# Hybrid attention and recurrent block on one core: the filler's first four output chunks by token halves, and v and differences loaded by pairs of units

## The chip, the cores and the metric

The kernel runs on one core of a Trainium2 chip. The metric is the device time of one execution in microseconds (us), given as the median of several runs. The engines are named as in the profile: PE is TensorE's matmuls and PEld its weight loads, DVE is VectorE, ACT is ScalarE, POOL is GpSimd and SP is SyncE, which here only issues DMAs.

## The reference

The block takes 1024 tokens of width 1024. It normalizes them, projects them once to all inputs of two branches, and joins the branches:

```
h = rmsnorm(x, norm_g) * (1 + scale) + shift
q, k, v, g_attn, xr, g_rnn, m_attn, m_rnn = split(h @ w_in)
y_attn = window_attention(rope(q), rope(k), v, sinks) * silu(g_attn)   # 16 heads of 64, 4 kv heads, window 128
y_rnn  = rg_lru(conv(xr)) * silu(g_rnn)
merged = sigmoid(m_attn) * (y_attn @ w_attn_proj) + sigmoid(m_rnn) * (y_rnn @ w_rnn_proj)
out    = rmsnorm(x + gate * (merged @ w_out), final_g)
```

All of it is float32. Each large matmul is made of three products: an operand is split into a high part h and a remainder l, and h·h, l·h and h·l are summed.

## The kernel before, in words

Tokens lie on the free axis, channels on the 128 partitions. After the normalization comes the input projection, in pairs of column groups (L711); its last pair is still open when attention begins. Then the attention loop runs over 35 steps, `for u in range(32 + 3)`. A unit u is one block of 128 queries of one of four head groups; n = u % 8 is its block. The engines' programs are written out by hand: every call appends to its engine's program, and each engine works through its own in that order.

Step u of the loop puts these on the engines:

- PE: the scores of unit u (`scores`, L1338, 8 matmuls), one piece of filler (12 matmuls), the transposes of unit u-2 (`transposed`, L1372, tile pt), the values of unit u-3 (`values`, L1408, tile pv).
- ACT and DVE: maximum, exponential and division (L1345 to L1365, tile p), then the split of the transposed weights into phc (ACT, L1377) and plc (DVE, L1383).
- POOL: the sinks of unit u+1 (COPY, L1326), the masks of unit u-2 (four selects into pm, L1394, none for a unit with u % 8 = 0), the loads of differences `load_d` (vd) and of values `load_v` (vb) for unit u+1, and, last, whatever remainders wl (L112) are due: `later_d` collects them and `do_later` puts them out at the end of the step. `smr_d` are stores that POOL issues.
- SP: the key and query load of a pair of units, `load_kq(m)`, issued at every odd u for units u+3 and u+4 (tiles ks, 384 KB, and qs, 512 KB). kq2, issued at u = 1, serves units 4 and 5; the loads for units 10 and 12 are issued at u = 7 and 9. All DMA calls go through a helper and have its line, L63.

The filler is a generator, `fill`. Its first six pieces (u = 0 to 5) are the last products of the input projection. `at_slot(s_last + 2, ...)` hangs calls on them, one per piece. From u = 6 on the pieces are those of `rp_steps`: y_rnn @ w_rnn_proj, in 8 output chunks c of 128 channels and for all 1024 tokens. A piece of before, `part(c, kc2)`, does two of the eight contraction chunks kc for one output chunk and both halves of the tokens (L175), so an output chunk takes four pieces. y_rnn lies in DRAM as yh and yl, eight chunks of 512 KB each; `load_y(c)` loads both parts of chunk c, the first two chunks in quarters of 256 KB into tiles that the input projection has left (hha, hla). `load_r(e)` loads the weights of output chunk e as two halves of 256 KB (tile r), and `prep_r(e, i)` splits half i: a cast to wh on ACT (L106) and the remainder wl on POOL while the attention loop runs. Half 0 serves kc 0 to 3, half 1 kc 4 to 7. `finish(c)` copies an output chunk out and stores it. After the attention branch's own filler, `load_b` brings the weights of w_out through a buffer pool, hpool, that also holds the split attention output (`a_alloc`).

The list that hangs loads on the first pieces reads, in before:

```
    at_slot(s_last + 2, ("N", 0, 0, lambda: load_r(0)), ("N", 0, 0, lambda: load_y(0)),
            ("N", 0, 0, lambda: load_r(1)), ("N", 0, 0, lambda: load_y(1)),
            ("N", 0, 0, lambda: prep_r(0, 0)), ("N", 0, 0, lambda: prep_r(1, 0)))
```

Of the kernel before, what the change touches and what calls it, by code (L numbers as in the profile page):

```python
# [13 lines left out]
F32R = mybir.dt.float32r  # L14
# [8 lines left out]
P = 128  # L23
S = 1024
# [31 lines left out]
def tile_hybrid_block(ctx, tc, x, pk, rows, posr, posi, c_row, w_ss, w_gate, w_main, w_v,  # L56
# [14 lines left out]
    def pool(st, name, bufs=1, **kw):  # L71
        return st.enter_context(tc.tile_pool(name=name, bufs=bufs, reuse_waits="tile", **kw))
# [1209 lines left out]
    at_ctx, psx_ctx = ExitStack(), ExitStack()  # L1282
    at = psx = None
    U = {}

    def open_attn():
        nonlocal at, psx
        psm_ctx.close()
        psx = pool(psx_ctx, "psx", space=PSUM)
        W["kq", 1] = pool(at_ctx, "kq1", side="right")  # L1290
        W["pp"] = pool(at_ctx, "pp", bufs=3, side="right")
        W["pp"].tile([P, 64], F32, name="pad", bufs=1)
        W["neg"] = W["pp"].tile([P, 8], F32, name="neg", bufs=1)
        G.memset(W["neg"][:], -1e30)
        for nm in ("vb", "hl", "yo"):
            W[nm] = pool(at_ctx, nm, side="right")
        at = pool(at_ctx, "at", side="right")
        load_kq(1)
        for u in range(4):
            load_v(u)  # L1300
            load_d(u)

# [9 lines left out]
        U["kq", m] = ks, qs  # L1312

    def load_v(u):
        vb = U["v", u] = W["vb"].tile([P, P], F32R, tag="vb", name="vb", bufs=5)
        dma(vb[:], vs_d[u // 8][:, u % 8, :], G)

    def load_d(u):
        if u % 8:
            vd = U["d", u] = at.tile([P, 2, P], F32R, tag="vd", name="vd", bufs=4)  # L1320
            dma(vd[:], dv_d[u // 8][:, u % 8, :, :].unsqueeze(0).to_broadcast([2, 64, 2, P]), G)

    def sink(u):
        px = U["p", u] = W["pp"].tile([P, 4, P + 1], F32, tag="p", name="p")
# [129 lines left out]
    def load_y(c):
        if c < 2:
            hs, ls = [[t[2 * c + i][0] for i in range(2)] for t in (hh, hl)]
            for i in range(2):
                dma(hs[i], yh_d[c][:, SL[i]])
                dma(ls[i], yl_d[c][:, SL[i]])
            yh[c], yl[c] = hs, ls  # L1460
            return
        h_ = W["yp"].tile([P, S], F32R, tag="Y", name="yh")
        l_ = W["yp"].tile([P, S], F32R, tag="Y", name="yl")
        dma(h_[:], yh_d[c])
        dma(l_[:], yl_d[c])
        yh[c] = [h_[:, SL[0]], h_[:, SL[1]]]
        yl[c] = [l_[:, SL[0]], l_[:, SL[1]]]

    def rp_steps():
        h_ctx.close()  # L1470
        pb_ctx.close()
        psr = pool(ps_ctx, "psr", space=PSUM, side="right")
        rp_acc.extend(psr.tile([P, S], F32, name=f"rp{i}") for i in range(2))
        W["yp"] = pool(ctx, "ypool", bufs=12)
        W["tout"] = pool(ctx, "tout", bufs=1)
        W["hpool"] = pool(ctx, "hpool", bufs=6)
# [18 lines left out]
        load_y(2)  # L1495
        load_y(3)
        for i, (c, k) in enumerate(seq):
            part(c, k)
            if i in (1, 2, 3, 4):
                load_y(i + 3)  # L1500
            if i in (1, 2):
                prep_r(i - 1, 1)
            if i in (6, 10):
                finish(0 if i == 6 else 1)
            if i >= 8 and k == 1 and c > 2:
# [10 lines left out]
    def a_alloc():
        U["al", 0] = W["hpool"].tile([P, 2, S], F32R, tag="L", name="al", bufs=1)
        for nm, g in (("ah", 0), ("ah", 1), ("al", 1), ("ah", 2), ("al", 2), ("ah", 3)):
            U[nm, g] = W["hpool"].tile([P, 2, S], F32R, tag="H", name=nm)
        for lst, nm in ((AH, "ah"), (AL, "al")):  # L1520
            lst.extend([[U[nm, g][:, a, t_] for t_ in SL] for a in range(2)]
                       for g in range(NG) if (nm, g) in U)
        t = [W["hpool"].tile([P, HALF], F32R, name="al6", bufs=1)]
        t += [wp.tile([P, HALF], F32R, tag="ws", name="al7", bufs=3) for i in range(3)]
        AL.append([[t[2 * a + i][:] for i in range(2)] for a in range(2)])
# [6 lines left out]
    def a_prep(m):  # L1532

        g, t0 = m // 4, (m % 4) * 256
        y = U.pop(("yq", m))

        def f1():
            gq = U.pop(("gq", m))
            V.tensor_tensor(out=y[:], in0=y[:], in1=gq, op=ALU.mult)

        def f2():
            if not AH:
                a_alloc()
# [12 lines left out]
        return f1, f2, f3  # L1556
# [138 lines left out]
    for u in range(32 + 3):  # L1695
# [233 lines left out]
    wt3 = load_b(4, hpool, "H")  # L1929
# [6 lines left out]
    w22 = load_b(5, hpool, "H")  # L1936
# [134 lines left out]
```

## Time and profile before

| | |
|---|---|
| median of 3 runs | 910.31 us (909.93 to 912.0) |
| the profiled execution's own time | 907.51 us |
| its span, first to last instruction | 905.8 us |
| mean granted TensorE clock | 0.997 |
| PE busy | 891.5 us (98%) |
| DVE, ACT, POOL busy | 718.2, 568.1, 185.1 us |
| DMA | 182.94 MB, mean 202 GB/s |

The page and the views come from one profiled execution. A row of a timeline has its start and length in us, the engine, the line, the operation, the tiles written and read, their shapes, a count, and in square brackets the idle time of the engine just before it with what ended it. The granted clock is a share of full speed. The DMA share is the busy share of the core's 16 DMA engines.

### The profile page before, as it was taken

How to read it: one execution, taken by the hardware profiler on the slowest of the kernel's cores; microseconds unless marked ns; L12 is line 12 of the kernel's file. 1: busy time of each engine (PE TensorE's matmuls, PEld its weight loads, DVE VectorE, ACT ScalarE, POOL GpSimd, SP SyncE). 2: the span in 40 equal slices, each digit the busy share in tenths (PEclk: the TensorE clock that was granted, in tenths of full speed). 3: DMA queues.
4: the chain of work that ended last, by engine and by line, in shares of the span. 5: the costliest groups of instructions: out<-in, count | busy, mean ns of one | idle time of the engine just before them, and what ended most of it. 6: DMA issues, size and time to landing. Idle time of an engine off the chain costs nothing.

```text
span 905.8 us, 12857 instructions
## 1 busy us (share of the span) xinstructions
PE 891.5 (98%) x4314; PEld 746.1 (82%) x4315; DVE 718.2 (79%) x1063; ACT 568.1 (63%) x1098; POOL 185.1 (20%) x331
## 2 busy tenths in 40 slices
PE   9999999999999999999999999998999999999997
PEld 6789888888888888888888888887888888888886
DVE  6988597989859875987789598898999836678855
ACT  7965564655557855786485884887888733115535
POOL 6420241200000000000000002596887720000000
PEclk9999999999999999999999999999999999999999
DMA  9829479873533353354446358999777389416504
GB/s 356 337 69 286 163 257 292 278 218 128 179 134 141 126 208 132 126 181 163 160 143 214 105 198 248 352 340 285 204 226 220 119 302 349 148 61 232 209 1 185
DMA packets 94837, 182.94 MB, mean 202 GB/s; under 512 B 15618, under 2 KB 36114, under 8 KB 94772
## 3 DMA queue, kind: packets, MB, share of 16 engines
q1 hardware_dynamic: 83200, 167.07, 53.4%
q0 software_dynamic: 11424, 14.80, 6.0%
q8 instruction: 34, 0.56, 0.3%
q14 instruction: 31, 0.25, 0.1%
q10 hardware_dynamic: 148, 0.27, 0.1%
HBM read 123.17 MB, written 59.21 MB: 201 GB/s over the span
## 4 chain that ended last, share of the span: by engine, by line
PE 91%; DVE 3%; DMA 3%; ACT 1%; POOL 1%; issue 1%; DVEq 0%; ACTq 0%; SPq 0%
PE bk L711 48%; PE rp L175 13%; PE out L1874 6%; PE pmain L175 5%; PE pgate L1027 5%; PE s_ps L1338 3%; PE bk L487 3%; PE pmain L487 2%; PE pv L1408 2%; DMA r<-w_rp 1%; DMA yl<-yl_d 1%; PE pt L1372 1%; PE pmain L1581 1%; PE pmain L1580 1%; PE pmain L1579 1%; PE bk L258 1%
## 5 line engine op out<-in xcount | busy, mean ns | idle before, releaser
L711 PE MATMUL bk<-nh,wh 128*128 128x512 f32 x368 | 143.3, 389 | 0.0
L711 PE MATMUL bk<-nl,wh 128*128 128x512 f32 x368 | 143.2, 389 | 0.0
L711 PE MATMUL bk<-nh,wl 128*128 128x512 f32 x368 | 98.4, 389 | 0.0
L106 ACT CAST wh<-r 128x512 fp32r<-128x512 f32 x107 | 65.5, 618 | 27.2 <-PE rp L175 12.8
L711 PEld LDWEIGHTS bk<-nh,wl 128*128 128x128 f32 x368 | 69.1, 188 | 14.4
L711 PEld LDWEIGHTS bk<-nh,wh 128*128 128x128 f32 x368 | 69.1, 188 | 14.2
L711 PEld LDWEIGHTS bk<-nl,wh 128*128 128x128 f32 x368 | 69.1, 188 | 14.2
L112 DVE TENSOR_TENSOR wl<-r,wh 128x512 fp32r<-128x512 f32 x91 | 62.0, 689 | 23.3 <-ACT wh L106 23.2
L63 POOL DMA_DIRECT2D yh_d<-av x1 | 0.6, 568 | 357.0 <-ACT av L1094 357.0
L711 PE MATMUL bk<-hl,wh 128*128 128x512 f32 x184 | 71.6, 389 | 0.0
L711 PE MATMUL bk<-hh,wh 128*128 128x512 f32 x184 | 71.6, 389 | 0.0
L112 DVE TENSOR_TENSOR wl<-ws,wh 128x512 fp32r<-128x512 f32 x76 | 52.0, 684 | 11.3 <-ACT wh L106 11.2
L106 ACT CAST wh<-ws 128x512 fp32r<-128x512 f32 x76 | 45.9, 614 | 7.2 <-PE bk L711 3.5
L1358 ACT ACTIVATE p<-p,small 128x129 f32<-128x129 f32 x128 | 50.0, 396 | 0.0
L711 PE MATMUL bk<-hh,wl 128*128 128x512 f32 x184 | 49.2, 389 | 0.0
L1338 PE MATMUL s_ps<-ks,qs 128*128 128x256 f32 (+1 forms) x256 | 35.8, 282 | 4.9 <-DVE yq L1427 3.0
L711 PEld LDWEIGHTS bk<-hh,wl 128*128 128x128 f32 x184 | 34.5, 188 | 7.2
L711 PEld LDWEIGHTS bk<-hh,wh 128*128 128x128 f32 x184 | 34.6, 188 | 7.1
L711 PEld LDWEIGHTS bk<-hl,wh 128*128 128x128 f32 x184 | 34.5, 188 | 7.1
L1338 PEld LDWEIGHTS s_ps<-ks,qs 128*128 128x128 f32 x256 | 32.8, 190 | 7.0 <-DVE yq L1427 3.5
L711 PE MATMUL bk<-hha,wh 128*128 128x512 f32 x92 | 35.8, 389 | 0.0
L711 PE MATMUL bk<-hla,wh 128*128 128x512 f32 x92 | 35.8, 389 | 0.0
(379 smaller groups left out, 2382.3 us busy)
## 6 DMA issues: line engine op xcount, KB each, us to landing
r<-w_main SPq DMA_DIRECT2D x100, 256.0 KB, 4.2
wada<-w_ss SPq DMA_DIRECT2D x16, 512.0 KB, 9.0
qs<-q_d SPq DMA_DIRECT2D x16, 512.0 KB, 7.5
wo_d<-wr SPq DMA_DIRECT2D x28, 256.0 KB, 2.5
wo<-wo_d SPq DMA_DIRECT2D x14, 512.0 KB, 6.2
ks<-k_d SPq DMA_DIRECT2D x12, 384.0 KB, 6.9
xt<-x SPq DMA_DIRECT2D x8, 512.0 KB, 6.8
sma_d<-c SPq DMA_DIRECT2D x16, 256.0 KB, 4.6
```

The costliest lines, as they stand in the source:

```text
L106: A.copy(dst[0][:], src)
L112: eng.tensor_tensor(out=dst[1][:], in0=src, in1=f32(dst[0][:]), op=ALU.subtract)
L175: mm = T.matmul(ps[hf], ww, xx[kc][hf], start=(kc == 0 and ww is w_h and xx is xh), stop=(kc == KC - 1 and xx is xl))
L258: T.matmul(bk[i % 2], zero[:, 0:P], zero, start=True, stop=True)
L487: T.matmul(starts[c][hf], ww[:, c0:c0 + P], xh[kc][hf], start=(kc == 0 and t_ == "h"), stop=(kc == KC - 1 and t_ == "l"))
L711: W["pe"] = T.matmul(ps, ww[:, kc * P:(kc + 1) * P], b[kc][i], start=(first and n == 0), stop=(n == 11), skip_group_check=not first)
L1027: W["pe"] = T.matmul(ps[:, SL[hf]], ww[:, c0:c0 + P], xx_[:, SL[hf]], start=(ic == 0 and i == 0), stop=(ic == 1 and i == 2))
L1338: W["pe"] = T.matmul(o, qs[:, j, qc], ks[:, kb:n % 2 + 2, b, :], start=(b == 0), stop=(b == 1))
L1358: A.activation(px[:, j, :], px[:, j, :], AF.Exp, bias=sm[:, 0, j:j + 1], accum_out=sm[:, 1, j:j + 1])
L1372: W["pe"] = T.transpose(pt[:, :, j, :], px[:, j, 0:P], ident[:])
L1408: W["pe"] = T.matmul(pv[:, cols], w, t_[:, cols], start=(i == 0), stop=(i == len(m) - 1))
L1874: T.matmul(o, a[k][x_][:, p * P:(p + 1) * P], b[k][y_][:, cols], start=(first and k == 0 and i == 0), stop=(k == 3 and i == 2), skip_group ...
```

## The change

There are two edits. No matmul is added or taken away.

First, the filler does output chunks 0 to 3 together. A piece of after, `four(th, p, kc2)`, does two contraction chunks for two output chunks (p = 0: chunks 0 and 1, p = 1: chunks 2 and 3) and one token half th: again 12 matmuls (L1503 to L1505). All of token half 0 comes first, so `load_y(c, th)` loads halves of 256 KB; those of chunks 0 to 3 for th = 0 go into hha and hla. The weights of chunks 2 and 3 stay on the chip over both token halves, in a tile o2 that lies where the attention output will lie later (printed below with a number, o_5945). The loads are hung on earlier pieces: `early(e)` loads the weights of chunk e and the first token half of two y chunks, and both calls come at the first two places of the list above, so their preparations move up two places as well. Chunks 4 to 7 go as before.

Second, from unit 8 on `load_v` and `load_d` load two units at once, at odd u, from a pool vq; for the units 8, 16 and 24 differences are now loaded that nobody reads.

Where hpool was one pool of equal buffers, every buffer now has a name, and `load_b` takes them by a list of names; the order is the same.

The core of the diff:

```diff
+    def load_r(e, halves=(0, 1)):
     def load_v(u):
-        vb = U["v", u] = W["vb"].tile([P, P], F32R, tag="vb", name="vb", bufs=5)
-        dma(vb[:], vs_d[u // 8][:, u % 8, :], G)
+        n, vp = (1, W["vb"]) if u < 8 else (2, W["vq"])
+        vb = vp.tile([P, n, P], F32R, tag="vb", name="vb", bufs=5 if u < 8 else 4)
+        dma(vb[:], vs_d[u // 8][:, u % 8:u % 8 + n, :], G)
...
     def prep_r(e, i):
         def f1():
-            O[e, i] = slot()
+            if e in (2, 3):
+                if e == 2:
+                    W["o2"] = W["hpool"].tile([P, 2, 2, HALF], F32R, tag=("al2", "ah3")[i],
+                                              name="o2")
+                O[e, i] = W["o2"][:, e % 2, 0, :], W["o2"][:, e % 2, 1, :]
+            else:
+                O[e, i] = slot()
...
+        def four(th, p, kc2):
+            for c in (2 * p, 2 * p + 1):
+                acc = rp_acc[p][:, SL[c % 2]]
+                for kc in (2 * kc2, 2 * kc2 + 1):
+                    h, l = O[c, kc // 4]
+                    cols = slice(kc % 4 * P, kc % 4 * P + P)
+                    T.matmul(acc, h[:, cols], yh[kc][th], start=(kc == 0), stop=False)
+                    T.matmul(acc, l[:, cols], yh[kc][th], start=False, stop=False)
+                    W["pe"] = T.matmul(acc, h[:, cols], yl[kc][th], start=False,
+                                       stop=(kc == KC - 1))
...
-        seq = [(c, k) for k in range(4) for c in range(2)]
-        seq += [(c, k) for c in range(2, KC) for k in range(4)]
+        seq = [(p, k, th) for th in range(2) for p, k in (
+            (0, 0), (0, 1), (0, 2), (1, 0), (1, 1), (0, 3), (1, 2), (1, 3))]
+        seq += [(c, k, None) for c in range(4, KC) for k in range(4)]
+        o_at = {0: (1, 1), 1: (2, 0), 2: (3, 0), 4: (2, 1), 5: (3, 1)}
...
-    at_slot(s_last + 2, ("N", 0, 0, lambda: load_r(0)), ("N", 0, 0, lambda: load_y(0)),
-            ("N", 0, 0, lambda: load_r(1)), ("N", 0, 0, lambda: load_y(1)),
+    def early(e):
+        load_r(e)
+        load_y(2 * e, 0)
+        load_y(2 * e + 1, 0)
+
+    at_slot(s_last + 2, ("N", 0, 0, lambda: early(0)), ("N", 0, 0, lambda: early(1)),
             ("N", 0, 0, lambda: prep_r(0, 0)), ("N", 0, 0, lambda: prep_r(1, 0)))
...
-        if 3 <= u < 31:
+        if 3 <= u < 7:
+            load_d(u + 1)
+            load_v(u + 1)
+        if 7 <= u < 30 and u % 2:
             load_d(u + 1)
             load_v(u + 1)
```

Three places show what moves. A row has the line, the operation, the tile written and the tile read, and the shape.

The first is SP's program at the units 0 and 1, around the second key and query load (ks and qs). `r<-w_rp` are weight halves of the recurrent projection, hha and hla the y halves, wo_d and ga_d stores. Before:

```order
L63 DMA r<-w_rp 128x512 x2
L63 DMA wo_d_147<-wr 128x512
L63 DMA ga_d_100<-c 128x2x256
L63 DMA hha_165<-yh_d_117 128x512
L63 DMA hla_167<-yl_d_125 128x512
L63 DMA hha_169<-yh_d_117 128x512
L63 DMA hla_171<-yl_d_125 128x512
L63 DMA ks<-k_d 128x768
L63 DMA qs<-q_d_93 128x1024
L63 DMA r<-w_rp 128x512 x2
```

In the changed kernel the same stretch, from the row behind the first `r<-w_rp`, reads:

```order
L63 DMA hha_165<-yh_d_117 128x512
L63 DMA hla_167<-yl_d_125 128x512
L63 DMA hha_169<-yh_d_118 128x512
L63 DMA hla_171<-yl_d_126 128x512
L63 DMA wo_d_147<-wr 128x512
L63 DMA ga_d_100<-c 128x2x256
L63 DMA r<-w_rp 128x512 x2
L63 DMA hha_173<-yh_d_119 128x512
L63 DMA hla_175<-yl_d_127 128x512
L63 DMA hha_177<-yh_d_120 128x512
L63 DMA hla_179<-yl_d_128 128x512
L63 DMA ks<-k_d 128x768
```

The second pair of weight halves and four y halves, six transfers of 256 KB, now stand ahead of the load instead of behind it.

The second place is POOL's program at the units 7 and 8. Before, it does one remainder (wl) at the end of each unit, of output chunks 0 and 1:

```order
L1326 COPY p<-pk_t 128x4
L1394 AFFINE_SELECT pm<-phc 64x256 x2
L1394 AFFINE_SELECT pm<-plc 64x256 x2
L63 DMA vb<-vs_d_86 128x128
L112 TENSOR_TENSOR wl<-r,wh 128x512
L1326 COPY p<-pk_t 128x4
L1394 AFFINE_SELECT pm<-phc 64x256 x2
L1394 AFFINE_SELECT pm<-plc 64x256 x2
L63 DMA vd<-dv_d_90 128x1x256
L63 DMA vb<-vs_d_86 128x128
L112 TENSOR_TENSOR wl<-r,wh 128x512
```

In the changed kernel the stretch begins with the end of unit 6:

```order
L112 TENSOR_TENSOR wl<-r,wh 128x512 x2
L1333 COPY p<-pk_t 128x4
L1401 AFFINE_SELECT pm<-phc 64x256 x2
L1401 AFFINE_SELECT pm<-plc 64x256 x2
L63 DMA vd<-dv_d_90 128x1x512
L63 DMA vb<-vs_d_86 128x256
L112 TENSOR_TENSOR o_5945<-r,o_5945 128x512
L1333 COPY p<-pk_t 128x4
L1401 AFFINE_SELECT pm<-phc 64x256 x2
L1401 AFFINE_SELECT pm<-plc 64x256 x2
L112 TENSOR_TENSOR o_5945<-r,o_5945 128x512
```

The remainders of chunks 0 and 1 have moved to the end of unit 6, both at once; units 7 and 8 make those of chunks 2 and 3, and unit 8 has no loads.

The third place is PE's program in unit 9, the fourth piece of `rp_steps`, behind that unit's scores. Before, the piece goes on with output chunk 1, and its weights are those that were split two units earlier:

```order
L1338 MATMUL s_ps<-ks,qs 128x256 x8
L175 MATMUL rp_5778<-yh,wh 128x512 x2
L175 MATMUL rp_5778<-yh,wl 128x512 x2
L175 MATMUL rp_5778<-yl,wh 128x512 x2
L175 MATMUL rp_5778<-yh,wh 128x512 x2
L175 MATMUL rp_5778<-yh,wl 128x512 x2
L175 MATMUL rp_5778<-yl,wh 128x512 x2
L1372 MATMUL pt<-ident,p 128x2x64 x4
```

In the changed kernel the piece begins chunks 2 and 3. L1504 is the product with the remainder; the first six filler rows are of chunk 2, the next two of chunk 3:

```order
L1345 MATMUL s_ps<-ks,qs 128x256 x8
L1503 MATMUL rp_5778<-hha_165,o_5945 128x512
L1504 MATMUL rp_5778<-hha_165,o_5945 128x512
L1505 MATMUL rp_5778<-hla_167,o_5945 128x512
L1503 MATMUL rp_5778<-hha_169,o_5945 128x512
L1504 MATMUL rp_5778<-hha_169,o_5945 128x512
L1505 MATMUL rp_5778<-hla_171,o_5945 128x512
L1503 MATMUL rp_5778<-hha_165,o_5945 128x512
L1504 MATMUL rp_5778<-hha_165,o_5945 128x512
```

The second and the eighth filler matmul of unit 9 now read the remainders that stand at the ends of units 7 and 8 on POOL.

More of the change, by code (lines that the diff above doesn't have):

```diff
@@ L1296, in open_attn @@
             W[nm] = pool(at_ctx, nm, side="right")
-        at = pool(at_ctx, "at", side="right")
+        at = pool(at_ctx, "at", bufs=2, side="right")
         load_kq(1)
-        for u in range(4):
+        load_v(0)
+        for u in range(1, 4):
             load_v(u)
@@ L1314, in load_v @@
     def load_v(u):
-        vb = U["v", u] = W["vb"].tile([P, P], F32R, tag="vb", name="vb", bufs=5)
-        dma(vb[:], vs_d[u // 8][:, u % 8, :], G)
-    def load_d(u):
-        if u % 8:
-            vd = U["d", u] = at.tile([P, 2, P], F32R, tag="vd", name="vd", bufs=4)
-            dma(vd[:], dv_d[u // 8][:, u % 8, :, :].unsqueeze(0).to_broadcast([2, 64, 2, P]), G)
+        n, vp = (1, W["vb"]) if u < 8 else (2, W["vq"])
+        vb = vp.tile([P, n, P], F32R, tag="vb", name="vb", bufs=5 if u < 8 else 4)
+        dma(vb[:], vs_d[u // 8][:, u % 8:u % 8 + n, :], G)
+        for i in range(n):
+            U["v", u + i] = vb[:, i, :]
+    def load_d(u):
+        n, dp = (1, at) if u < 8 else (2, W["vq"])
+        vd = dp.tile([P, n, 2, P], F32R, tag="vd", name="vd", bufs=4)
+        dma(vd[:], dv_d[u // 8][:, u % 8:u % 8 + n, :, :].unsqueeze(0).to_broadcast(
+            [2, 64, n, 2, P]), G)
+        for i in range(n):
+            U["d", u + i] = vd[:, i, :, :]
     def sink(u):
@@ L1432, in tile_hybrid_block @@
     rp_acc, R, O = [], {}, {}
-    def load_r(e):
+    def load_r(e, halves=(0, 1)):
         src = w_rp[e] if e < KC else w_ap[e - KC]
-        R[e] = [load_half(src[:, SL[i]]) for i in range(2)]
+        for i in halves:
+            R[e, i] = load_half(src[:, SL[i]])
     later_a, later_d = [], []
@@ L1441, in f1 @@
         def f1():
-            O[e, i] = slot()
-            cast(O[e, i], R[e][i])
+            if e in (2, 3):
[5 more added lines that the diff above has]
+                O[e, i] = slot()
+            cast(O[e, i], R[e, i])
         later_a.append(f1)
-        later_d.append(lambda: rest(O[e, i], R[e][i], eng=G if "att" in W else V))
+        later_d.append(lambda: rest(O[e, i], R[e, i], eng=G if "att" in W else V))
         if "att" not in W:
@@ L1452, in do_later, with load_y @@
                 todo.pop(0)()
[L1454 to L1467, printed above, removed]
+    def load_y(c, th):
+        if c < 4 and not th:
+            h_, l_ = hh[c][0], hl[c][0]
+            yh[c], yl[c] = [h_], [l_]
+        elif c < 4:
+            if c % 2 == 0:
+                W["y1"] = [W["yp"].tile([P, S], F32R, tag="Y", name=n_) for n_ in ("yh", "yl")]
+            h_, l_ = [t[:, SL[c % 2]] for t in W["y1"]]
+            yh[c].append(h_)
+            yl[c].append(l_)
+        else:
+            if not th:
+                for y_, n_ in ((yh, "yh"), (yl, "yl")):
+                    t = W["yp"].tile([P, S], F32R, tag="Y", name=n_)
+                    y_[c] = [t[:, t_] for t_ in SL]
+            h_, l_ = yh[c][th], yl[c][th]
+        dma(h_, yh_d[c][:, SL[th]])
+        dma(l_, yl_d[c][:, SL[th]])
     def rp_steps():
@@ L1487, in f @@
                 A.copy(t[:], rp_acc[c % 2][:])
-                store(tr_d[c], t[:])
+                if th is None:
+                    store(tr_d[c], t[:])
+                else:
+                    for a in range(2):
+                        store(tr_d[2 * c + a][:, SL[th]], t[:, SL[a]])
             later_a.append(f)
@@ L1491, in finish @@
                 do_later()
-        seq = [(c, k) for k in range(4) for c in range(2)]
-        seq += [(c, k) for c in range(2, KC) for k in range(4)]
[L1495 to L1505, printed above, removed]
+        seq = [(p, k, th) for th in range(2) for p, k in (
+            (0, 0), (0, 1), (0, 2), (1, 0), (1, 1), (0, 3), (1, 2), (1, 3))]
+        seq += [(c, k, None) for c in range(4, KC) for k in range(4)]
+        y_at = {0: (6, 0), 1: (7, 0), 2: (0, 1), 3: (1, 1), 4: (2, 1), 5: (3, 1),
+                6: (4, 1), 7: (5, 1), 9: (6, 1), 10: (7, 1)}
+        r_at = {0: (3, 0), 1: (2, 1), 2: (3, 1)}
+        o_at = {0: (1, 1), 1: (2, 0), 2: (3, 0), 4: (2, 1), 5: (3, 1)}
+        out_at = {5: (0, 0), 8: (1, 0), 13: (0, 1), 17: (1, 1)}
+        prep_r(0, 1)
+        load_r(2, (0,))
+        load_y(4, 0)
+        load_y(5, 0)
+        for i, (c, k, th) in enumerate(seq):
+            if th is None:
+                part(c, k)
+            else:
+                four(th, c, k)
+            if i in y_at:
+                load_y(*y_at[i])
+            if i in r_at:
+                load_r(r_at[i][0], r_at[i][1:])
+            if i in o_at:
+                prep_r(*o_at[i])
+            if i in out_at:
+                finish(*out_at[i])
+            if i >= 20 and k == 1:
                 finish(c - 1)
-            if i % 4 == 2:
+            if i % 4 == 2 and i >= 10:
                 load_r((i + 2) // 4 + 1)
-            if i >= 4 and i % 4 < 2:
+            if i >= 12 and i % 4 < 2:
                 prep_r((i + 4) // 4, i % 4)
@@ L1514, in tile_hybrid_block, with a_alloc @@
     AH, AL = [], []
[L1516 to L1525, printed above, removed]
+    def a_alloc(g):
+        for nm in ("ah", "al"):
+            if nm == "al" and g == 3:
+                t = [W["hpool"].tile([P, HALF], F32R, name="al6")]
+                t += [wp.tile([P, HALF], F32R, tag="ws", name="al7", bufs=3) for i in range(3)]
+                AL.append([[t[2 * a + i][:] for i in range(2)] for a in range(2)])
+                continue
+            t = U[nm, g] = W["hpool"].tile([P, 2, S], F32R, tag=f"{nm}{g}", name=nm)
+            (AH if nm == "ah" else AL).append([[t[:, a, t_] for t_ in SL] for a in range(2)])
     def load_gq(m):
@@ L1541, in f2 @@
         def f2():
-            if not AH:
-                a_alloc()
+            if len(AH) == g:
+                a_alloc(g)
             A.copy(U["ah", g][:, :, t0:t0 + 256], y[:])
@@ L1755, in tile_hybrid_block @@
     at_ctx.close()
+    vq_ctx.close()
     psx_ctx.close()
@@ L1775, in tile_hybrid_block, with load_b @@
     ahh, alh = [[lst[c // 2][c % 2] for c in range(KC)] for lst in (AH, AL)]
-    in_l = []
-    def load_b(j, pool, tag):
+    places = [nm + str(g) for g in range(NG) for nm in ("ah", "al")][:7] * 2
+    def load_b(j, pool, tag=None):
         res = []
         for i in range(2):
-            if pool is hpool:
-                in_l.append(len(in_l) in (1, 8))
-                tag = "L" if in_l[-1] else "H"
             r = tpool.tile([P, 2, HALF], F32, tag="wr", name="wo32", bufs=2)
             dma(r[:], wo_d[j][2 * i:2 * i + 2].rearrange("k p n -> p k n"))
-            t = pool.tile([P, 2, 2, HALF], F32R, tag=tag, name="wo",
-                          bufs=1 if tag == "L" else None)
+            t = pool.tile([P, 2, 2, HALF], F32R, tag=tag or places.pop(0), name="wo")
             A.copy(t[:, 0], r[:])
@@ L1911, in result @@
         dma(out[t * P:(t + 1) * P, :], xo[t][:])
-    w21 = load_b(1, hpool, "H")
+    w21 = load_b(1, hpool)
     for t in range(4):
         load_x(t)
-    wt2 = load_b(2, hpool, "H")
+    wt2 = load_b(2, hpool)
     for p in range(4):
```

15 lines of the change are left out of this document (8 added, 7 removed).

## The prediction

> **What bounds the kernel now.** The busy line of the page comes first.
>
> ```profile
> span 905.8 us, 12857 instructions
> PE 891.5 (98%) x4314; PEld 746.1 (82%) x4315; DVE 718.2 (79%) x1063; ACT 568.1 (63%) x1098; POOL 185.1 (20%) x331
> ```
>
> TensorE works 891.5 of 905.8 us, so a change that keeps the matmuls, as this one does, can only move its 14.3 us of idle time. The windows of the attention loop tell where some of that lies (columns: window, its length, busy us of PE, PEld, DVE, ACT, POOL, granted clock, DMA share, GB/s).
>
> ```profile
> 557.00:590.00 33.00, 32.55 (x190) 28.20 (x190) 26.44 (x48) 24.82 (x79) 15.86 (x32) 1.00 1.04 337
> 590.00:625.00 35.00, 30.33 (x181) 25.86 (x180) 29.69 (x51) 26.08 (x83) 27.07 (x46) 1.00 1.06 329
> 625.00:700.00 75.00, 74.95 (x455) 65.60 (x454) 70.74 (x124) 65.10 (x204) 58.48 (x107) 1.00 0.75 219
> ```
>
> The clock is full. From 557 to 625 the DMA engines are busy throughout (share 1.04 and 1.06) and PE loses 0.45 and 4.67 us; from 625 on it loses nothing. The waits of PE in 557 to 625 give the releasers, and its timeline the places: the scores of units 4, 10 and 12.
>
> ```profile
> PE s_ps L1338 <- DVE yq L1427: 3.0, 1, 3.0
> PE s_ps L1338 <- DMA qs<-q_d: 1.4, 1, 1.4
> PE s_ps L1338 <- DVE p L1365: 0.5, 1, 0.5
> PE rp L175 <- DMA yl<-yl_d: 0.2, 1, 0.2
> ```
>
> ```profile
> 574.91 1.19 PE L1338 MATMUL s_ps<-ks,qs 128*128 128x256 f32 x8 [0.45 <-DVE p L1365]
> ...
> 606.02 1.19 PE L1338 MATMUL s_ps<-ks,qs 128*128 128x256 f32 x8 [1.37 <-DMA qs<-q_d]
> ...
> 618.76 1.19 PE L1338 MATMUL s_ps<-ks,qs 128*128 128x256 f32 x8 [3.04 <-DVE yq L1427]
> ```
>
> The wait of 3.04 is put down to VectorE, but the query transfers decide it. The two that units 10 and 12 read were issued, and landed, thus:
>
> ```profile
> 591.64 0.32 SPq L63 DMA_DIRECT2D qs<-q_d  x1
> DMA to landing us min/median/max: 14.2/14.2/14.2
> ```
>
> ```profile
> 607.18 0.32 SPq L63 DMA_DIRECT2D qs<-q_d  x1
> DMA to landing us min/median/max: 11.4/11.4/11.4
> ```
>
> 591.64 + 14.2 = 605.8, and unit 10 starts at 606.02; 607.18 + 11.4 = 618.6, and unit 12 starts at 618.76. Both queries came late through a full DMA, and the 0.22 us for yl is of the same kind.
>
> **Part 1: the second query and key load (kq2) goes behind six more transfers.** Unit 4 reads kq2. The change puts both weight halves of chunk 1 and the four y halves of chunks 2 and 3 ahead of it on SP, 6 x 256 KB = 1.573 MB, which stood behind it. SP's timeline, the landings, and the DMA rate:
>
> ```profile
> 566.67 0.32 SPq L63 DMA_DIRECT2D ks<-k_d  x1
> 568.48 0.32 SPq L63 DMA_DIRECT2D qs<-q_d  x1
> 569.29 1.40 SPq L63 DMA_DIRECT2D r<-w_rp  x2
> ```
>
> ```profile
> ks<-k_d SPq DMA_DIRECT2D x1, 384.0 KB, 6.9
> r<-w_rp SPq DMA_DIRECT2D x1, 256.0 KB, 6.2
> ```
>
> ```profile
> 568.00:570.00 2.00, 2.00 (x14) 1.72 (x13) 1.90 (x5) 1.94 (x8) 0.01 (x1) 1.00 1.07 384
> 570.00:572.00 2.00, 2.00 (x13) 1.78 (x13) 1.93 (x5) 1.60 (x5) 0.18 (x1) 1.00 1.03 396
> 572.00:574.00 2.00, 2.00 (x12) 1.68 (x12) 1.86 (x5) 2.00 (x8) 0.00 (x0) 1.00 1.00 366
> ```
>
> ks landed at 573.6, and the r behind qs at 569.29 + 6.2 = 575.5; its 256 KB take 0.7 us at the mean of 382 GB/s, so qs landed at about 574.8. Unit 4's scores began at 574.91, with PE free since 574.46: no slack at all. With 1.573 MB more ahead, kq2 lands 1.573 / 0.382 = 4.1 us later, and unit 4 waits **+4.1 us**. Nothing covers it: scores lead their unit, and PE runs in program order. Bounds: 4.7 us at the 337 GB/s of 557 to 590; below, 0, if the six do not delay kq2 (a rival below). I take 4.1, the rate of the very stretch.
>
> [...]
>
> **Part 2: two remainders that GpSimd makes too late for unit 9.** In the changed order the fourth filler step (unit 9) is the first on chunks 2 and 3, and its second and eighth matmuls read remainders (L112) that GpSimd makes at the ends of units 7 and 8, behind masks and loads. The rows of GpSimd and their neighbours:
>
> ```profile
> 600.54 0.65 POOL L1326 COPY p<-pk_t 128x4 f32<-128x4 f32 x1
> 601.15 0.89 POOL L1394 TENSOR_SCALAR_AFFINE_SELECT pm<-phc 64x256 fp32r<-64x256 f32 x2
> 602.10 0.89 POOL L1394 TENSOR_SCALAR_AFFINE_SELECT pm<-plc 64x256 fp32r<-64x256 f32 x2
> 602.94 0.83 POOL L63 DMA_DIRECT2D vd<-dv_d  x1
> 603.76 0.56 POOL L63 DMA_DIRECT2D vb<-vs_d  x1
> ```
>
> ```profile
> L112 POOL TENSOR_TENSOR wl<-r,wh x18: 1262/1294/1802, 583.7 to 733.0; 128x512 fp32r<-128x512 f32 x18
> ```
>
> ```profile
> 590.25 0.57 ACT L1377 CAST phc<-pt 128x512 fp32r<-128x512 f32 x1
> ```
>
> ```profile
> 584.85 0.95 PE s_ps L1338 x8
> 585.81 2.75 PE rp L175 x12
> ```
>
> ```profile
> 599.63 0.64 PE L1338 MATMUL s_ps<-ks,qs 128*128 128x256 f32 x4
> ```
>
> Per unit GpSimd needs 0.6 for the copy, 1.8 for four masks, 1.4 for the two loads, and 1.3 per remainder. Count from the start of unit 6 (584.85). The masks can start when the cast phc ends, at 590.82, so at 6.0. Unit 6 now ends with two remainders: 6.0 + 1.8 + 1.4 + 2.6 = 11.8. Unit 7: copy, masks, pair loads, remainder, 5.1, to 16.9. Unit 8, without loads: 0.6 + 1.8 + 1.3 = 3.7, to 20.6. PE reaches unit 9's scores at 599.63, so 14.8, its second filler matmul after 0.95 + 0.23 (2.75 / 12) at 16.0, and the eighth six matmuls (1.37) later at 17.3. GpSimd delivers at 16.9 and 20.6, so PE ends 20.6 - 17.3 = **+3.3 us** late. Below: if unit 8's masks wait for nothing but their own cast, it is 9.9 (unit 8, two thirds of 14.8) + 6.0 + 1.8 + 1.3 = 19.0, so 1.7. Above: all four remainders at the longest, 1.80, add 2.0, so 5.3. I take 3.3, from the median row. A pair load is costed as one issue: the 256 KB stores in the next fence issue in 0.55 each, no more than the smaller vb, so size does not set it.
>
> ```profile
> 591.25 1.10 POOL L63 DMA_DIRECT2D smr_d<-c  x2
> ```
>
> **Part 3: the same at unit 12.** The seventh step (unit 12) reads at its eighth matmul the remainder queued at the end of unit 11, again behind that unit's masks and loads. In before the same chain stands in unit 11:
>
> ```profile
> 614.65 0.60 PE L1372 MATMUL pt<-ident,p 128*128 128x128 f32 x4
> ```
>
> ```profile
> 620.23 1.30 POOL L112 TENSOR_TENSOR wl<-r,wh 128x512 fp32r<-128x512 f32 x1
> ```
>
> It ends at 621.53, 6.9 us after unit 11's transposes. PE, without its wait of 3.04, would be at the scores of unit 12 at 615.72, 1.1 after them, and at the eighth matmul after 1.1 + 0.95 + 0.23 + 1.37 = 3.6. So **+3.3 us**. Below: the bare work of GpSimd, 5.1, gives 1.5; above, a remainder of 1.80 gives 3.8.
>
> **Part 4: what goes.** Ahead of unit 10's query stand 256 KB less (0.7 us), ahead of unit 12's 1.573 MB less (4.1 us), since output chunks 0 to 3 first need only half of each y. PE also comes 4.1 and 7.4 us later than its old pace. So 1.37 + 3.04 + 0.22 go: **-4.6 us**. Late next are the remainders above.
>
> **At nothing.** The filler keeps 16 steps of 12 matmuls for the first four chunks, at the same 0.23 each. Pair loads spare GpSimd 1.4 us in every even unit from 8 on; after 625 it lies beside PE, which is full. If that cover went, nothing would be lost, as GpSimd only does less. The unused differences of units 8, 16 and 24 are 0.39 MB, 1.0 us of DMA where its share is 0.75; uncovered, at most that. The y halves are more issues at 0.32 on SP, less than the 0.7 that 256 KB take to move.
>
> **Sum.** 4.1 + 3.3 + 3.3 - 4.6 = +6.1. The profiled execution took 907.51 (span 905.8): 913.6. The median of the runs, 910.31, lies 2.8 above it: **916.4**.
>
> **Rivals.**
> - *Everything hidden, so faster.* The six transfers do not hold up kq2, and GpSimd delivers by 16.0 and 17.3. Of the waits only 1.37 - 0.7 = 0.7 at unit 10 stays, as PE comes on time: -3.9, 906.4. It decides wherever the new waits together stay below 2 us. For it: the wait at unit 4 before is booked on p, not on a transfer. Against it: a DMA share of 1.0 ahead of unit 4, and a GpSimd with 11.8 us of work by the end of unit 6. Chance 0.14.
> - *kq2 in time, GpSimd late.* The transfers in flight are not served in turn, so the six do not cost kq2 their whole length: 3.3 + 3.3 - 4.6 = +2.0, 912.3. Against it: ks, issued at 566.67, landed at 573.6 and r, issued 2.6 later, at 575.5, in turn. Chance 0.15. [...]
> - *kq2 late, GpSimd in time.* The 4.1 us at unit 4 let GpSimd get ahead, or the masks run earlier than in the rows: 4.1 - 4.6 = -0.5, 909.8. Against it: the remainders of unit 8 wait for a cast made in unit 8. Chance 0.16.
> - *As forecast*: 0.55.
>
> **How the numbers follow.** A measurement of this kernel can tell 0.2%, 1.8 us, from no change. The low ends, with kq2 in time, are 0 + 1.7 + 1.5 - 4.6 = -1.4, 908.9; the high ends 4.7 + 5.3 + 3.8 - 4.6 = +9.2, 919.5. The range 908.9 to 919.5 leaves out the first rival, 0.14, and little else. Faster than 908.5: the first rival and a fifth of the third, 0.17. Within 908.5 to 912.1: the rest of the third and a third of the second, 0.18. Slower: the rest, 0.65.
>
> **What would show it.** Right: unit 4's scores wait 4 us for qs; SP's kq2 has the six transfers ahead of it; in unit 9 the lines that replace L175 wait about 1 us and then 2 us for GpSimd's remainder, in unit 12 about 3 us; no wait for qs at units 10 and 12. Wrong: unit 4 starts at 575, so part 1 falls; no wait of PE for GpSimd, so parts 2 and 3 fall; or units 10 and 12 still wait for queries, so part 4 does. The whole is wrong if the idle of PE in 557 to 640 is below the 5.1 us of before.

## The result and the profile after

| | before | after |
|---|---|---|
| median | 910.31 us | 920.17 us (918.47 to 920.3) |
| the profiled execution's own time | 907.51 us | 920.09 us |
| its span | 905.8 us | 918.0 us |
| mean granted clock | 0.997 | 0.994 |

The ratio is 1.0114, interval 1.01 to 1.0128: the change is slower by 10.4 us by the ratio, by 9.9 us between the two medians. The forecast was slower by 6.1, with 919.5 as the upper end. A fourth run of the kernel before, 991.15 us, lies 80.8 us above the median of the other three and is left out.

The busy line of the page shows the first surprise. PE has the same 4314 matmuls as before, but is busy for 895.9 us, where it was 891.5. Of the 12.2 us by which the span grew, 7.8 are idle time of PE and 4.4 are matmuls that took longer.

```profile
PE 895.9 (98%) x4314; PEld 748.3 (82%) x4315; DVE 721.1 (79%) x1063; ACT 567.4 (62%) x1098; POOL 170.2 (19%) x310
```

The list of waits of TensorE (PE) in 557 to 640 us of the changed kernel has those that were forecast, and no others but 0.2 us. The queries of units 10 and 12 are gone from it.

```profile
PE rp L1504 <- POOL o L112: 6.0, 3, 3.0
PE s_ps L1345 <- DMA qs<-q_d: 5.5, 1, 5.5
PE pv L1415 <- POOL pm L1401: 0.2, 1, 0.2
```

PE's timeline has them at unit 4's scores, at the second and the eighth filler matmul of unit 9, and at the eighth of unit 12:

```profile
579.40 2.05 PE L1345 MATMUL s_ps<-ks,qs 128*128 128x256 f32 x8 [5.54 <-DMA qs<-q_d]
...
610.34 0.50 PE L1504 MATMUL rp<-hha,o 128*128 128x512 f32 x1 [1.13 <-POOL o L112]
...
613.94 0.51 PE L1504 MATMUL rp<-hha,o 128*128 128x512 f32 x1 [1.94 <-POOL o L112]
...
631.79 0.50 PE L1504 MATMUL rp<-yh,o 128*128 128x512 f32 x1 [2.98 <-POOL o L112]
```

Unit 4's eight score matmuls took 2.05 us, where they took 1.19 before. The windows of the same stretch show that it ran at a lower clock (window, length, busy us of PE, PEld, DVE, ACT, POOL, granted clock, DMA share, GB/s). The clock column is no longer 1.00 throughout.

```profile
557.00:590.00 33.00, 27.45 (x141) 23.47 (x140) 20.05 (x35) 18.95 (x61) 10.81 (x22) 0.90 0.86 268
590.00:625.00 35.00, 31.54 (x185) 26.38 (x185) 30.18 (x50) 27.21 (x87) 25.59 (x44) 1.00 1.00 303
625.00:640.00 15.00, 12.01 (x62) 10.10 (x61) 10.95 (x21) 9.11 (x29) 6.76 (x13) 0.89 0.81 256
```

Cut at the moments at which the clock changes, the two drops look thus:

```profile
575.08:578.50 3.42, 0.00 (x0) 0.00 (x0) 0.81 (x2) 0.58 (x1) 3.16 (x7) 1.00 1.02 340
578.50:581.91 3.41, 2.51 (x10) 2.45 (x11) 0.00 (x0) 0.43 (x1) 0.82 (x1) 0.50 1.08 401
581.91:585.32 3.41, 3.41 (x9) 2.64 (x9) 3.09 (x6) 1.70 (x9) 0.00 (x0) 0.50 0.60 165
585.32:588.74 3.42, 3.42 (x25) 3.12 (x25) 1.32 (x3) 1.64 (x4) 1.09 (x4) 1.00 0.04 14
```

```profile
629.70:633.11 3.41, 1.32 (x6) 1.04 (x7) 2.44 (x4) 1.52 (x7) 1.97 (x3) 1.00 0.92 271
633.11:636.52 3.41, 3.41 (x18) 3.41 (x17) 0.79 (x2) 1.32 (x3) 0.94 (x3) 0.50 0.72 254
636.52:639.93 3.41, 3.41 (x20) 2.87 (x20) 3.20 (x7) 2.14 (x9) 0.89 (x3) 1.00 0.67 228
```

A stretch of 3.41 us in which PE worked 0.00 or 1.32 us is followed by half clock, for two stretches the first time and one the second. In the kernel before, the longest wait, 3.04 us, fell across two such stretches (edges in steps of 3.413 us from a drop of its clock at 23.46 us; another, at 904.10, is 258 such steps behind that), and with 1.75 and 2.04 us of work in them the clock stayed full:

```profile
613.97:617.39 3.42, 1.75 (x10) 1.14 (x8) 3.25 (x6) 2.86 (x10) 1.73 (x4) 1.00 1.05 296
617.39:620.80 3.41, 2.04 (x13) 1.90 (x14) 2.14 (x5) 0.94 (x4) 2.88 (x6) 1.00 1.08 282
```

GpSimd (POOL) in the changed kernel made its remainders late, as was worked out: the two of unit 6 in one go, then those that units 9 and 12 wait for. Masks of unit 7 (pm) stand between them; the second row of them, shown here, took 1.57 us, where the prediction's row has 0.89.

```profile
601.66 2.98 POOL L112 TENSOR_TENSOR wl<-r,wh 128x512 fp32r<-128x512 f32 x2
...
606.03 1.57 POOL L1401 TENSOR_SCALAR_AFFINE_SELECT pm<-plc 64x256 fp32r<-64x256 f32 x2
...
609.02 1.26 POOL L112 TENSOR_TENSOR o<-r,o 128x512 fp32r<-128x512 f32 x1
...
612.62 1.26 POOL L112 TENSOR_TENSOR o<-r,o 128x512 fp32r<-128x512 f32 x1
...
630.47 1.26 POOL L112 TENSOR_TENSOR o<-r,o 128x512 fp32r<-128x512 f32 x1
```

### The profile page after: what moved, and what is told of

The parts are those of the page before. It is cut to its first block, busy times and chain, and to the rows that moved or that the text cites. A ratio compares the mean times of both kernels' runs of the same rounds, so it can differ in the third digit from the quotient of the medians.

```text
span 918.0 us, 12851 instructions
## 1 busy us (share of the span) xinstructions
PE 895.9 (98%) x4314; PEld 748.3 (82%) x4315; DVE 721.1 (79%) x1063; ACT 567.4 (62%) x1098; POOL 170.2 (19%) x310
## 5 line engine op out<-in xcount | busy, mean ns | idle before, releaser
L711 PEld LDWEIGHTS bk<-nl,wh 128*128 128x128 f32 x368 | 69.6, 189 | 14.3
L106 ACT CAST wh<-r 128x512 fp32r<-128x512 f32 x103 | 63.0, 618 | 28.6 <-PE pmain L175 9.6
L711 PE MATMUL bk<-hl,wh 128*128 128x512 f32 x184 | 71.6, 389 | 0.0
L711 PE MATMUL bk<-hh,wh 128*128 128x512 f32 x184 | 71.6, 389 | 0.0
L1384 ACT CAST phc<-pt 128x512 fp32r<-128x512 f32 x32 | 18.7, 586 | 32.5 <-PE pv L1415 16.3
```

The source lines that it names most:

```text
L106: A.copy(dst[0][:], src)
L711: W["pe"] = T.matmul(ps, ww[:, kc * P:(kc + 1) * P], b[kc][i], start=(first and n == 0), stop=(n == 11), skip_group_check=not first)
L1384: A.copy(phc[:], U["t", u][0])
```

## The experiments

Each was timed against runs of the kernel before on the same chip (medians of it 909.06, 909.52, 909.25 and 908.38 in the four sessions). The changed kernel itself was timed only in the first session, with 910.31 for the kernel before, so a gain against its 920.17 is read from two sessions; the ratios to the kernel before are the safer measure. Two theories stood against each other for the size: the waits bring half clock with them, or something else in the change costs the rest.

**1. kq2 first.** The second `early` call and chunk 1's preparation go behind the second query and key load.

```diff
-    at_slot(s_last + 2, ("N", 0, 0, lambda: early(0)), ("N", 0, 0, lambda: early(1)),
-            ("N", 0, 0, lambda: prep_r(0, 0)), ("N", 0, 0, lambda: prep_r(1, 0)))
+    at_slot(s_last + 2, ("N", 0, 0, lambda: early(0)), ("N", 0, 0, lambda: None),
+            [("N", 0, 0, lambda: early(1)), ("N", 0, 0, lambda: prep_r(0, 0))],
+            ("N", 0, 0, lambda: None), ("N", 0, 0, lambda: prep_r(1, 0)))
```

> The changed kernel with the second early call (weights of chunk 1, first token half of y chunks 2 and 3) put behind the second query and key load, and chunk 1's preparation two pieces later. Theory A (kq2 lands late behind six transfers, and the idle time of 5.5 us lets the granted clock fall to half for 6.8 us): the wait for qs at unit 4 (5.54) falls to about 0.45 and the half clock behind it goes, so 5.1 + 2.7 = 7.8 us less than the changed kernel's 920.2: 912.4. Theory B (the half clock has another cause than that wait): 5.1 less, 915.1. Theory C (kq2 is not late because of the six): no change, 920.

Measured 913.01 (912.78 to 913.3), ratio 1.0042 (1.0027 to 1.0058): 7.2 us less than the changed kernel, or 6.5 by the two ratios. The time alone lies between theories A and B; the trace is A's. PE waits 1.1 us for qs instead of 5.5, and the same 6.0 for the remainders, so that part is independent. The drop behind unit 12 is left: half clock from 626.09 to 629.50, behind a stretch with 1.34 us of work. That none is left at units 4 and 5 is an estimate from the mean granted clock of the profiled execution, 0.997 where the changed kernel has 0.994.

```profile
PE rp L1504 <- POOL o L112: 6.0, 3, 2.9
PE s_ps L1345 <- DMA qs<-q_d: 1.1, 1, 1.1
```

**2. The remainders of chunks 2 and 3 on VectorE.**

```diff
-        later_d.append(lambda: rest(O[e, i], R[e, i], eng=G if "att" in W else V))
+        later_d.append(lambda: rest(O[e, i], R[e, i], eng=G if "att" in W and e not in (2, 3) else V))
```

> The changed kernel with the four remainders of output chunks 2 and 3 made by VectorE instead of GpSimd. Theory A (units 8, 9 and 12 wait for a GpSimd that is late): the waits for the remainders (6.0 in all), unit 8's loss of 1.5 and the half clock behind unit 12's wait (1.9) go, 9.5 less; the four subtractions of 0.69 on VectorE cost between 0 and 2.8: 910.7 to 913.5. Theory B (TensorE would be late there anyway, for the casts or for the queries): less than 4 us gained, 916 or more.

Measured 916.88 (913.97 to 918.78), ratio 1.0083 (1.0063 to 1.0102): 3.3 us gained (2.8 by the ratios), where theory A wanted 6.7 to 9.5. The profile is of an execution of 913.97 us, the lowest of six. In it the wait of unit 12 for a remainder is gone, but VectorE is late too for unit 9, and a wait of 1.1 us for the query of unit 12 came back:

```profile
PE s_ps L1345 <- DMA qs<-q_d: 6.0, 2, 4.9
PE rp L1504 <- DVE o L112: 2.1, 1, 2.1
```

So another engine alone does not remove the waits. Unit 8's loss, which I had put down to these four, stayed as well (unit 8 to 9 took 6.26 us, 6.28 in the changed kernel, 4.77 before): the two remainders of unit 6, on which it rests, are of chunks 0 and 1 and were still on GpSimd.

**3. Both.**

> Both edits together. Theory A: 920.2 - 7.8 - 9.5 + (0 to 2.8) = 902.9 to 905.7, faster than the kernel before by 5 to 7 us. Theory B (a faster TensorE runs into the queries of units 10 and 12 again): a wait for qs of 0.7 or more returns there, 906 to 910.

Measured 910.09 (908.11 to 911.07), ratio 1.0006 (0.9996 to 1.0017), 4 us above theory A and level with the kernel before. It lies at the upper end of theory B, but without B's sign, as no wait for qs is left. PE waits 3.5 us for VectorE's remainders, and a stretch with 2.1 us of idle time (1.30 us of work) is again followed by half clock, from 607.3 to 610.8 us.

```profile
PE rp L1504 <- DVE o L112: 3.5, 2, 2.1
PE s_ps L1345 <- DVE plc L1390: 1.2, 1, 1.2
```

**4. Work in the wait.** The changed kernel with idle matmuls ahead of unit 4's scores, on the keys and queries of the pair before; the scores overwrite what they write.

```diff
+        if u == 4:
+            ko, qo = U["kq", 1]
+            for i in range(36):
+                T.matmul(s_ps[:, i % 4, :], qo[:, i % 4, 0:P], ko[:, 0:2, 0, :],
+                         start=True, stop=True)
```

> The changed kernel with 36 more matmuls of the scores' shape ahead of unit 4's scores; they read keys and queries of the pair before and write what the scores overwrite. They fill 36 x 0.12 = 4.3 us of the 5.5 us in which TensorE waits for qs. Theory A (the idle time itself lowers the clock): the granted clock stays at 1.00 through units 4 and 5, and though there is more work, the time falls by 2.7 us, to 917.5. Theory B (something else lowers it): no gain, 920 or more.

Measured 917.96 (915.98 to 922.32), ratio 1.0095 (1.0075 to 1.0115). 2.2 us less, but with a range too wide to tell, and the theory's own sign is missing. The profile, of an execution of 922.32, has the clock falling to half at unit 4 still, behind a stretch with 1.21 us of work, as 2.2 us of wait remained in it:

```profile
577.97:581.38 3.41, 1.21 (x10) 1.03 (x10) 0.00 (x0) 0.00 (x0) 1.66 (x2) 1.00 1.05 346
581.38:584.79 3.41, 3.41 (x12) 2.83 (x11) 1.76 (x3) 2.14 (x9) 0.00 (x0) 0.50 0.88 287
```

So I filled the whole wait, with 52 (`range(52)` in the diff):

> As the fourth experiment, with 52 instead of 36 idle matmuls ahead of unit 4's scores: 52 x 0.12 = 6.2 us, more than the whole wait. Theory A (a stretch of the clock's grid with some 2 us of idle time lowers the clock): no half clock at units 4 and 5, scores 0.9 us later than in the changed kernel, unit 5 at 585.2 instead of 587.0, so 1.8 us less than 920.2: 918.4, with more work. Theory B (the half clock is not the answer to idle time): 0.9 us more, 921.

Measured 919.04 (917.06 to 920.08), ratio 1.0099 (1.0079 to 1.0119). The time alone does not settle it; the windows and the timeline do. From 573 to 587 us PE has no idle time, the clock stays full, and unit 5's scores start at 584.97, where 585.2 was expected and 587.04 is the changed kernel's: 2.1 us earlier with 52 matmuls more. So idle time is what lowers the clock there: with 0.00 us of work in a stretch it was 0.50 in the changed kernel, with work throughout 1.00.

```profile
576.50:580.00 3.50, 3.50 (x31) 3.44 (x29) 0.00 (x0) 0.00 (x0) 2.84 (x4) 1.00 1.02 374
580.00:583.50 3.50, 3.50 (x21) 3.08 (x20) 1.51 (x3) 2.13 (x9) 0.00 (x0) 1.00 0.90 268
```

```profile
584.97 1.12 PE L1350 MATMUL s_ps<-ks,qs 128*128 128x256 f32 x8
```

The same scores in the changed kernel:

```profile
587.04 1.12 PE L1345 MATMUL s_ps<-ks,qs 128*128 128x256 f32 x8
```

The profiled execution, at 920.08, is no faster for it: the clock fell again behind a later wait and was 0.50 from 613.38 to 616.79, behind a stretch with 1.51 us of work, where the changed kernel has 1.00. The waits for remainders are the same 6.0 us, but they fell otherwise on the 3.41 us stretches: in the changed kernel the least work in one at unit 9 was 1.66 us, from 609.22 to 612.63.

**5. Preparation one step earlier.** This is the first experiment, and in addition chunks 0 and 1 get their second halves prepared at units 3 and 5, and chunks 2 and 3 theirs one unit earlier; all remainders stay on GpSimd.

```diff
-        o_at = {0: (1, 1), 1: (2, 0), 2: (3, 0), 4: (2, 1), 5: (3, 1)}
+        o_at = {0: (2, 0), 1: (3, 0), 3: (2, 1), 4: (3, 1)}
-        prep_r(0, 1)
...
+            ("N", 0, 0, lambda: prep_r(0, 1)), ("N", 0, 0, lambda: prep_r(1, 0)),
+            ("N", 0, 0, lambda: prep_r(1, 1)))
```

> The changed kernel with kq2 ahead of the second early call, as in the first experiment, and with the preparation of the second halves of chunks 0 and 1 and of both halves of chunks 2 and 3 one step earlier; the remainders stay on GpSimd, which stood idle for 7.2 us at unit 5. Theory A (the remainders are late only because they are queued late): from the 913.0 of the first experiment go unit 8's loss (1.6), the waits of unit 9 (3.1) and unit 12 (2.9) and the half clock behind it (1.9): 903.5, faster than the kernel before by 5. Theory B (a faster TensorE meets the queries of units 10 and 12 or the casts again): up to 5 of the 9.5 come back, 904 to 909. Theory C (GpSimd is short of time, not late in order): no better than 911.

Measured 909.02 (907.15 to 911.52), ratio 0.9997 (0.9985 to 1.0009): theory B's time, though not by the waits that it named. No wait for a remainder is left, so the order on GpSimd was the point; but a new wait stands there, for the values of a pair load:

```profile
PE pv L1415 <- DMA vb<-vs_d: 3.3, 1, 3.3
PE pv L1415 <- POOL pm L1401: 0.9, 2, 0.7
```

**6. The six transfers alone, in the kernel before.**

```diff
-    at_slot(s_last + 2, ("N", 0, 0, lambda: load_r(0)), ("N", 0, 0, lambda: load_y(0)),
-            ("N", 0, 0, lambda: load_r(1)), ("N", 0, 0, lambda: load_y(1)),
+    at_slot(s_last + 2, [("N", 0, 0, lambda: load_r(0)), ("N", 0, 0, lambda: load_y(0))],
+            [("N", 0, 0, lambda: load_r(1)), ("N", 0, 0, lambda: load_y(1))],
+            ("N", 0, 0, lambda: None), ("N", 0, 0, lambda: None),
```

> The kernel before, with nothing changed but that the loads of chunk 1's weights and of y chunk 1 stand ahead of the second query and key load instead of behind it: the same six transfers. Theory A: unit 4 waits 5 us for qs, the half clock adds 2.7 or 1.3 by where the wait falls in the clock's windows, and the old waits of units 10 and 12 (4.6) are swallowed, as the transfers gain what TensorE loses: +1.8 to +3.2, 911 to 912.3. Theory B (the queries of units 10 and 12 stay late): +6.4 to +7.8, 915.5 to 917. Theory C (the order of the loads does not matter): 909.1.

Measured 915.33 (912.72 to 917.63), ratio 1.0066 (1.0049 to 1.0084), 6.0 us more: between the theories, closer to B. Unit 4 waits 6.2 us, and the clock is half from 577.06 to 587.30, as expected. Of the old waits unit 10's is swallowed, unit 12's is not, so that PE comes later is not enough to remove that one. Nor do fewer bytes ahead of it seem enough: in experiment 2, where the bytes are those of the changed kernel and PE is less late, 1.1 us of it came back.

```profile
PE s_ps L1338 <- DMA qs<-q_d: 6.2, 1, 6.2
PE s_ps L1338 <- DVE yq L1427: 3.1, 1, 3.1
```

**7. The pair loads alone, in the kernel before** (the diff's `load_v`, `load_d` and their calls).

> The kernel before with values and differences loaded by pairs of units from unit 8 on, alone. Theory A: TensorE never waits for GpSimd there, so nothing: 909.1, within 0.2%. [...] Theory C (the unused differences and the larger transfers press on a full DMA, and the queries of units 10 and 12 come later): 0.5 to 1 us slower.

Measured 913.46 (913.2 to 914.48), ratio 1.0046 (1.0033 to 1.0059): 4 us slower, more than any theory had. The second edit is not free. Unit 12's query, issued at 606.7 (607.2 in the kernel before), now lands after 16.1 us instead of 11.4. The mean granted clock of the profiled execution is 0.995, that of the kernel before 0.997, and the wait for the query grows from 3.0 to 6.6:

```profile
PE s_ps L1345 <- DMA qs<-q_d: 6.6, 1, 6.6
```

A pair's difference load, the first, takes 16.9 us from issue to landing:

```profile
vd<-dv_d POOLq DMA_DIRECT2D x1, 256.0 KB, 16.9
```

**8. The same bytes at the same places, as single transfers.** The lines are against experiment 7; tiles and transfers are again of one unit each.

```diff
-            load_d(u + 1)
-            load_v(u + 1)
+            for w in (u + 1, u + 2):
+                load_d(w)
+                load_v(w)
```

> The kernel before with the loads of the pair version at the same places, with the same bytes (unused differences too), but each unit's load as a DMA of its own. Theory A (the form matters: a pair's transfer is slow and holds up the others): like the kernel before, 909.5. Theory B (bytes asked for one unit earlier press on a full DMA ahead of unit 12's query): like the pair version, 913.5.

Measured 910.6 (909.63 to 912.05), ratio 1.0016 (1.0006 to 1.0025): 1.4 us, nearer to A. About a third of the cost of pairs is that bytes are asked for earlier; about two thirds go when each unit's load is a transfer of its own. Unit 12's query lands after 13.2 us here. The two single difference loads land after 12.6 us:

```profile
vd<-dv_d POOLq DMA_DIRECT2D x2, 128.0 KB, 12.6
```

**9. Single loads in the changed kernel.**

> The changed kernel with values and differences loaded singly again, as before. Theory A (a queue on GpSimd sets units 9 and 12): unit 8's end has two more issues of 1.4 us ahead of the remainder that unit 9 waits for, so +1.4; unit 11 has as many as it had: 921.6. Theory B (GpSimd is not what unit 9 waits for, or a pair costs what two singles cost): no change, 920.2.

Measured 921.11 (920.49 to 921.56), ratio 1.0127 (1.0113 to 1.0142). The mechanism is there (the second wait of unit 9 grows from 1.94 to 3.39 us, all three waits for remainders from 6.0 to 6.6), but the intervals of this and of the changed kernel overlap, so the size is not settled. In the changed kernel pair loads are neither clearly better nor clearly worse.

**10. Experiment 5 with single loads.**

> The fifth experiment (kq2 first, preparation one step earlier) with values and differences loaded singly. Theory A (a pair load lands late and is what TensorE waited for there, 3.3 us for vb and 0.9 for masks): 4 us less than its 909.0, 905, faster than the kernel before by about 4.5; the two more issues in even units cost GpSimd 1.4 us, which the earlier preparation leaves room for. Theory B (the wait only moves on, to the queries of units 10 and 12): 908 to 909.5.

Measured 904.58 (904.05 to 906.86), ratio 0.9951 (0.9935 to 0.9966): theory A to half a microsecond. It is the first version faster than the kernel before, by 4.5 us, and it no longer has the second edit. PE loses 1.2 and 1.4 us in the two stretches, and the clock is full in both:

```profile
557.00:590.00 33.00, 31.81 (x185) 27.44 (x184) 27.03 (x46) 25.55 (x80) 18.04 (x34) 1.00 1.04 328
590.00:625.00 35.00, 33.65 (x200) 28.89 (x198) 33.20 (x57) 29.74 (x94) 30.07 (x51) 1.00 1.07 323
```

**11. y chunk 1 behind kq2 too**, to take away the last wait for qs at unit 4 (1.1 us).

> The version with kq2 first, earlier preparation and single loads, with one step more of the same: the two halves of y chunk 1 also go behind the second query and key load. Theory A (each 256 KB ahead of kq2 costs its 0.7 us until the wait is gone): the wait of 1.1 for qs at unit 4 goes, 903.5. Theory B (unit 4 is then held by the maxima of unit 2 or by its own softmax chain): 904.6, no change. Theory C (y chunk 1 now lands too late for unit 6): 905 or more.

Measured 904.65 (904.03 to 904.93), ratio 0.9952 (0.9939 to 0.9966): no change. The wait at unit 4 went (unit 4 starts 4.71 us behind unit 3, not 5.94), and PE lost about as much again over units 5 to 12: it waits 0.5 us for the query of unit 6 and 1.3 us for the softmax chain on VectorE. That is theory B in effect, though not at the place it named.

## Why the prediction was wrong

The direction, the three places and the four waits were right; the size was not. The span grew by 12.2 us, and so did the stretch from the scores of unit 3 to those of unit 14 (59.4 to 71.6 us), where 6.1 were forecast. Against the terms of the sum:

- *The clock, not in the sum.* This is the step that failed. The prediction read "The clock is full" off the rows of before, took it that the change "can only move its 14.3 us of idle time", and priced every wait at its own length. Half clock followed the wait of 5.54 us for two stretches, and unit 4 took 7.64 us instead of 4.93, 2.7 more. It followed unit 12's wait of 2.98 for one stretch, and cost 1.3 us in that unit and 0.6 in the next. Together this is 4.6 us, three quarters of the 6.1 us by which the span outgrew the forecast, and it agrees with the 4.4 us by which PE's busy time grew. Experiment 4 with 52 matmuls shows the cause, since added work kept the clock full and brought unit 5 forward.
- *Part 1, +4.1.* Unit 4 came 5.1 us later. Experiments 1 and 6 show that the order of these transfers is the cause. The step that put 1.573 MB at 382 GB/s took too high a rate: 340 GB/s were moved in the stretch from 575.08, and 305 in the one before it, which would give 4.6 to 5.2. That the rate is all of the difference is not shown.
- *Part 2, +3.3.* The two waits of unit 9 are 1.13 + 1.94 = 3.1. That this is so close is in part luck. GpSimd delivered 18.4 and 22.0 us behind unit 6's scores, where the prediction has 16.9 and 20.6, and PE reached unit 9 at 16.0, where it has 14.8: the two errors nearly cancel.
- *Unit 8, not in the sum.* PE was late because unit 8 lost 1.5 us. The two remainders of unit 6 took 1.49 us each, not 1.29, and unit 8's filler, which reads them, took 3.5 us instead of 2.8; the masks behind them came late as well, for the other half. I took the lag of unit 6 as free of cost for the units between.
- *Part 3, +3.3.* Measured 2.98.
- *Part 4, -4.6.* All went, as said, and with them 0.5 us that unit 7 lost before to late masks. Experiment 6 corrects the reason for unit 12's: PE's delay would not have been enough.
- *At nothing: the pair loads.* That they were free was wrong by 4 us in the kernel before (experiment 7), by the DMA and not by GpSimd. In the changed kernel no such cost shows (experiment 9).

So measured, 5.1 + 3.1 + 1.5 + 3.0 + 4.6 - 4.6 - 0.5 = 12.2.

The median came closer to the forecast than the span did, 920.17 for 916.4, and that is luck too. The prediction added 2.8 us from the profiled execution to the median; the changed kernel has 920.09 and 920.17. The runs of the kernel before in the later sessions go with the granted clock: the 19 at a mean clock of 0.992 have a median of 910.2 us, the 18 at 0.996 one of 908.4. So the kernel before seems to lose clock too in part of its executions, and the profiled one, at 907.51, lost none in the attention loop. No profile shows where.

The first rival, everything hidden, had it that new waits below 2 us decide; experiment 10 comes near that case (waits of 2.5 us in all), reached by moving loads and preparations and without pair loads, not by the change as it stands. The other two rivals fall: kq2 was late by 5.5 us and GpSimd by 6.0. The remark that pair loads leave GpSimd more time fits experiment 9, but is not what decides.

What stays open is why a pair's transfer holds the others up: 12.6 against 16.9 us to its own landing with the same bytes, and 13.2 against 16.1 for unit 12's query, are shown, their cause is not.

## What to carry to other kernels

Price a new wait with the clock that follows it: a wait of some 3 us cost its length here (3.04 us before) or 1.9 us more (2.98 us after), by where it fell, and one of 5.5 us cost 2.7 more. A load list in which every byte is needed soon is a schedule: 1.573 MB ahead of a load that is read next cost 5.1 us here, where the DMA share was 0.89, 1.02 and 1.08 in the three stretches from 571.67 to 581.91. A change that relieves one resource (bytes of y ahead of the queries) shows its worth only when its own new work is queued early enough; here the same filler order was some 10 us slower or 4.5 us faster, by the order of a dozen calls and the form of two loads.

## What the runs showed of the hardware

In the attention loop the granted clock fell to 0.50 in whole stretches of 3.41 us. Within a run they lay on one grid: the three drops of the changed kernel, the last at its end, begin at 578.50, 633.11 and 916.42 us, 16 and 83 steps of 3.413 apart. After a stretch with 0.00 us of PE work (the changed kernel) or 1.21 to 1.39 (experiments 1, 3, 4 and 6 and the changed kernel) it was half; after 1.66 (the changed kernel) and 1.75 (the kernel before) it was full. In between the runs differ: 1.47 us left it full in the fifth experiment, and 1.51 in the version with 52 matmuls did not. It was full again after a stretch without idle time (3.41 us of work, the changed kernel and the third experiment); 2.51 (the changed kernel) and 2.61 (experiment 6) did not bring it back. The grid's edges lie elsewhere in each run (at 578.50 in the changed kernel, at 581.38 in experiment 4, at 577.06 in experiment 6), so equal waits cost unequal times: one of 3.04 us cost no clock in the kernel before, one of 2.98 cost 1.9 us beyond its length in the changed kernel.
